# Hybrid transformer block on one core: softmax weights left unscaled in attention, and turned by a product with a diagonal of their factors that GpSimd makes

## The chip, the cores and the metric

The kernel runs on one core of a Trainium2 chip. The metric is the device time of one execution in microseconds. Most executions of it agree within 0.3%.

## The reference, cut to what matters

Two layers work on 768 tokens (256 of context, 512 latent), 1024 channels each. Every layer has three mixers side by side: a two-way recurrence (RWKV-7), grouped attention and a state space model. Their outputs are merged, and a feed-forward block follows. The attention is:

```python
def grouped_attend(q, k, v):
    s = jnp.einsum('bqhgd,bkhd->bhgqk', q, k).astype(jnp.float32) * ATTN_SCALE
    p = jax.nn.softmax(s, axis=-1).astype(v.dtype)
    return jnp.einsum('bhgqk,bkhd->bqhgd', p, v)
```

There are 16 query heads of 64 channels in 4 groups that share keys and values. In both layers the 512 latent queries see all 768 keys. In the first layer alone the 256 context queries see the 256 context keys too.

## The kernel before, in words

Attention is cut into jobs of four query tiles of 128 queries. A latent job (T job) is one head with its four tiles against 768 keys; a context job (C job, first layer only) holds two heads with two tiles each against 256 keys. The first layer has 16 T jobs and 8 C jobs, the second 16 T jobs: 40 in all.

`front` makes the scores of a job in PSUM (`pS`, L1176 and L1177; a T job has its keys in two halves of 384), takes the largest of each row (`st`, L1179), and lets ScalarE write the exponentials into `P` with their row sums (L1180). As each half of a T job is taken against its own maximum, some small operations on `st` (L1184 to L1190) turn sums and maxima into one factor for each row and half, `st[:, 1, y, x]`. A C job needs the reciprocal alone (L1192). Then `P` is multiplied by that factor in place: tiles 0 and 2 on VectorE (L1199), tiles 1 and 3 on ScalarE (L1197).

`back` takes a job's keys 128 at a time (`turn`): TensorE transposes the four tiles of `P` against the identity into one PSUM bank (`pPT`, recorded at L312, the line of a helper that issues calls in a row), ScalarE rounds that to `ph` (L1213), VectorE takes the rest as `pl` (L1214), and two matmuls with `V` add into `pO`. A T job has six turns, 24 transposes; a C job two turns, 8 transposes. With 32 T jobs and 8 C jobs that makes 832 transposes in 208 turns.

`back` of a job and `front` of the next advance by turns. Both are steps of a filler that the recurrence (`rwkv`, its matmuls `pSk`, `pSb`, `pRU`, `pS`, `pY`, and the read-out `rwkv_out` with `pcen`, `pv`, `pr`) calls between its own steps. The attention stage is therefore also that of the recurrence. The order on each engine is made at build time by a scheduler that plays the program through; each engine then runs its own list strictly in that order. GpSimd's list (POOL) holds in this stage the loads of keys, values and queries (`kT`, `kl`, `V`, `qT`), the inverse of small triangular blocks during the recurrence's first step (L1463 and L1465, 62 products and differences in a layer) and the clearing of its results (`XTi`, L1478). TensorE takes float32 operands in `pkb` (L1348), a product of 128x128 by 128 columns in the preparation of the recurrence: 48 calls, and two records for each call in the trace.

Of the kernel before, what the change touches and what calls it, by code (L numbers as in the profile page):

```python
# [8 lines left out]
F32 = mybir.dt.float32  # L9
F32R = mybir.dt.float32r  # L10
I32 = mybir.dt.int32
AF = mybir.ActivationFunctionType
ALU = mybir.AluOpType
# [140 lines left out]
class Net:  # L154
# [975 lines left out]
    def attend(self, l, A, yb, ctx_out, es):  # L1130

        nc, v = self.nc, self.nc.vector
        p = self.pool(f"at_{l}", es=es, side="right")
        pS = self.pool(f"atS_{l}", 2, PSUM, es, side="right")
        pO = self.pool(f"atO_{l}", 1, PSUM, es, side="right")
        ident = self.c["ident"]
        t0 = 0 if ctx_out else TC

        def group(g):
            kT = p.tile([128, T], F32R, name="kT", bufs=2)  # L1140
            nc.gpsimd.dma_start(kT, A["k"][g])
            kl = p.tile([128, T], F32R, name="kl", bufs=2)
            nc.gpsimd.dma_start(kl, A["kl"][g])
            V = p.tile([128, 6, 128], F32R, name="V", bufs=2)
            nc.gpsimd.dma_start(V, A["v"][g])
            return dict(g=g, kT=kT, kl=kl, V=V, qT={}, yo={})
# [10 lines left out]
        def front(g, qts, nk, Ps):  # L1157

            if g not in groups:
                groups[g] = group(g)  # L1160
            G = groups[g]
            qT, kT, kl = G["qT"], G["kT"], G["kl"]
            for h, _ in qts:
                if h not in qT:
                    qT[h] = p.tile([128, T], F32R, name="qT", bufs=3)
                    nc.gpsimd.dma_start(qT[h][:, t0:], A["q"][4 * g + h, :, t0:])
            nh = 2 if nk == T else 1
            w = nk // nh
            st = p.tile([128, 3, nh, 4], F32, name="st", tag=f"st{nh}", bufs=2)
            for x, (h, o) in enumerate(qts):  # L1170
                P = p.tile([128, T], F32, name="P", tag="P", bufs=8)
                Ps.append(P)
                for y in range(nh):
                    ps = pS.tile([128, 512], F32, name="pS", tag="pS")
                    ks = slice(w * y, w * y + w)
                    nc.tensor.matmul(ps[:, :w], qT[h][:, o:o + 128], kT[:, ks], start=True, stop=False)  # L1176
                    nc.tensor.matmul(ps[:, :w], qT[h][:, o:o + 128], kl[:, ks], start=False, stop=True)  # L1177
                    nm, sm, _ = (st[:, z, y, x:x + 1] for z in range(3))
                    v.reduce_max(nm, ps[:, :w], axis=AX.X, negate=True)  # L1179
                    nc.scalar.activation(P[:, ks], ps[:, :w], AF.Exp, bias=nm, accum_out=sm)  # L1180
                yield
            if nh == 2:
                mm = p.tile([128, 2, 4], F32, name="mm", bufs=2)
                v.tensor_tensor(mm[:, 0], st[:, 0, 0], st[:, 0, 1], op=ALU.min)  # L1184
                v.tensor_sub(st[:, 2], mm[:, 0:1].to_broadcast([128, 2, 4]), st[:, 0])
                nc.scalar.activation(st[:, 2], st[:, 2], AF.Exp)
                v.tensor_mul(st[:, 1], st[:, 1], st[:, 2])
                v.tensor_add(mm[:, 1], st[:, 1, 0], st[:, 1, 1])
                v.reciprocal(mm[:, 1], mm[:, 1])
                v.tensor_mul(st[:, 1], st[:, 2], mm[:, 1:2].to_broadcast([128, 2, 4]))  # L1190
            else:
                v.reciprocal(st[:, 1], st[:, 1])  # L1192
            for x in range(4):
                for y in range(nh):
                    ks = slice(w * y, w * y + w)
                    if x % 2:
                        nc.scalar.activation(Ps[x][:, ks], Ps[x][:, ks], AF.Copy, scale=st[:, 1, y, x:x + 1])  # L1197
                    else:
                        v.tensor_scalar(Ps[x][:, ks], Ps[x][:, ks], st[:, 1, y, x:x + 1], None, op0=ALU.mult)  # L1199
            yield  # L1200

        def back(g, qts, nk, Ps):
# [3 lines left out]

            def turn(kt):
                pt = pO.tile([128, 512], F32, name="pPT", tag="pPT", bufs=2)
                self.row_of([self.later(nc.tensor.transpose, pt[:, 128 * x:128 * x + 128],
                                        Ps[x][:, 128 * kt:128 * kt + 128], ident) for x in range(4)])  # L1210
                ph = p.tile([128, 512], F32R, name="ph", bufs=2)
                pl = p.tile([128, 512], F32R, name="pl", bufs=2)
                nc.scalar.copy(ph, pt)  # L1213
                v.tensor_sub(pl, pt, ph)  # L1214
                return ph, pl

            nxt = turn(0)
            for kt in range(nk // 128):
                ph, pl = nxt
# [9 lines left out]
            if nk == T:  # L1229
                if h % 2 == 0:  # L1230
                    yo[h // 2] = p.tile([128, 512], F32, name="yo", bufs=2)
                y = yo[h // 2]
# [3 lines left out]
            else:  # L1236
                y = p.tile([128, 256], F32, name="yoc")
# [8 lines left out]
        for job in jobs + [None]:  # L1246
            Ps = []
# [1043 lines left out]
```

## Time and profile before

| what | value |
|---|---|
| median of 2 runs | 3452.74 us (3449.69 to 3455.78) |
| the profiled execution's own time | 3449.99 us |
| its span, first to last instruction | 3448.1 us |
| mean granted TensorE clock | 0.954 of 2.4 GHz |
| attention with recurrence, first layer | 735 to 1137 us of the span |
| attention with recurrence, second layer | 2570 to 2895 us of the span |

The two stages take 727 of 3448 us. PE is TensorE's matmul, PEld its weight load, DVE is VectorE, ACT ScalarE, POOL GpSimd, SP the engine that issues most DMAs. The end of a matmul is modelled in the trace, so the distance from one start to the next tells more than its duration.

### The profile page before, as it was taken

To read this page: it belongs to the slowest core of one execution; us is meant where nothing else is said; L and a number is where in the kernel's file an instruction comes from. 1 tells how busy PE (TensorE), PEld (TensorE's weight loads), DVE (VectorE), ACT (ScalarE), POOL (GpSimd) and SP (SyncE) were. 2 spreads that over 40 slices of the span, in tenths; PEclk is the share of its full clock that TensorE was granted. 3 is DMA by queue.
4 is the path that set the end of the run, shared out by engine and by line. 5 is a ranking of instruction groups with operands and counts; after the bars stand their busy time and mean duration, and the time that the engine had idled before them with its cause. 6 is when DMAs were issued, how large, how long until landed. Compare 5 with 4: busy or idle time off the path is not lost.

```text
span 3448.1 us, 63260 instructions
## 1 busy us (share of the span) xinstructions
PE 3209.1 (93%) x24501; PEld 2671.1 (77%) x24501; DVE 2217.1 (64%) x4618; ACT 1555.5 (45%) x3166; POOL 524.3 (15%) x746
## 2 busy tenths in 40 slices
PE   7999998979998899999999899978979998999998
PEld 6888897967775789888888787767867775787776
DVE  3889368847778545665455746548858786564446
ACT  3444456656677313422122444436657674243222
POOL 0002022214000030122100221102224000201000
PEclk9999999979999999999999999988969999999999
DMA  5545465675533544344333466637656535544332
GB/s 194 165 135 161 157 186 183 183 204 137 134 93 129 173 130 152 99 147 151 107 109 126 155 207 199 198 110 214 193 169 168 140 86 163 160 152 147 128 128 87
DMA packets 429668, 522.41 MB, mean 152 GB/s; under 512 B 238132, under 2 KB 304820, under 8 KB 428728
## 3 DMA queue, kind: packets, MB, share of 16 engines
q1 hardware_dynamic: 409608, 461.84, 43.9%
q0 software_dynamic: 19760, 56.52, 5.4%
q8 instruction: 194, 3.18, 0.4%
q14 instruction: 106, 0.87, 0.1%
HBM read 372.78 MB, written 145.46 MB: 150 GB/s over the span
## 4 chain that ended last, share of the span: by engine, by line
PE 72%; DVE 10%; DMA 9%; ACT 4%; issue 3%; SPq 1%; POOL 1%; DVEq 0%; ACTq 0%; POOLq 0%
PE pf L343 4%; PE pf L344 4%; PE ph L333 4%; PE pf L345 4%; PE ph L335 4%; PE ph L334 4%; PE pO L312 2%; PE pc L333 2%; PE pga L333 2%; PE pc L334 2%; PE pc L335 2%; PE pga L334 2%; PE pga L335 2%; PE pm L333 2%; PE pm L334 2%
## 5 line engine op out<-in xcount | busy, mean ns | idle before, releaser
L238 ACT CAST whi<-wraw 128x1024 fp32r<-128x1024 f32 x288 | 293.5, 1048 | 571.7 <-PE pf L345 157.5
L239 DVE TENSOR_TENSOR wlo<-wraw,whi 128x1024 fp32r<-128x1024 f32 x288 | 356.0, 1255 | 250.1 <-ACT whi L238 243.9
L333 PE MATMUL ph<-xh,whi 128*128 128x512 f32 (+1 forms) x832 | 287.7, 347 | 4.8 <-DVE xTf L1887 3.6
L334 PE MATMUL ph<-xl,whi 128*128 128x512 f32 (+1 forms) x832 | 286.4, 345 | 0.7 <-DVE xl L1889 0.7
L335 PE MATMUL ph<-xh,wlo 128*128 128x512 f32 (+1 forms) x832 | 285.7, 344 | 0.0
L343 PE MATMUL pf<-whi,hh 128*128 128x512 f32 x640 | 253.4, 397 | 0.7 <-DVE ff L1977 0.3
L344 PE MATMUL pf<-wlo,hh 128*128 128x512 f32 x640 | 252.9, 396 | 0.9 <-DVE wlo L239 0.9
L345 PE MATMUL pf<-whi,hl 128*128 128x512 f32 x640 | 250.7, 396 | 0.0
L1179 DVE TENSOR_REDUCE st<-pS 128x1 f32<-128x384 f32 x288 | 151.7, 535 | 100.9 <-PE pS L1177 98.7
L333 PE MATMUL pga<-xh,whi 128*128 128x512 f32 (+1 forms) x576 | 211.5, 367 | 1.6 <-ACT kT L1063 1.6
L335 PE MATMUL pga<-xh,wlo 128*128 128x512 f32 (+1 forms) x576 | 209.2, 363 | 0.2 <-DVE wlo L239 0.2
L334 PE MATMUL pga<-xl,whi 128*128 128x512 f32 (+1 forms) x576 | 209.2, 363 | 0.0
L1180 ACT ACTIVATE P<-pS,st 128x384 f32<-128x384 f32 x288 | 164.2, 572 | 77.7 <-DVE st L1179 69.5
L1977 DVE TENSOR_TENSOR ff<-ff,pf 128x512 f32<-128x512 f32 x132 | 89.3, 686 | 154.5 <-PE pf L345 154.1
L333 PEld LDWEIGHTS ph<-xh,whi 128*128 128x128 f32 x832 | 157.7, 190 | 30.0 <-issue 6.2
L334 PEld LDWEIGHTS ph<-xl,whi 128*128 128x128 f32 x832 | 158.1, 190 | 22.1 <-DVE xl L1889 1.1
L335 PEld LDWEIGHTS ph<-xh,wlo 128*128 128x128 f32 x832 | 157.7, 190 | 20.4
L1214 DVE TENSOR_TENSOR pl<-pPT,ph 128x512 fp32r<-128x512 f32 x208 | 141.2, 684 | 38.8 <-ACT ph L1213 37.3
L333 PE MATMUL pm<-yh,whi 128*128 128x512 f32 (+1 forms) x384 | 141.7, 373 | 22.1 <-ACT whi L238 16.3
L1176 PE MATMUL pS<-kT,qT 128*128 128x384 f32 x288 | 128.4, 446 | 26.0 <-ACT P L1180 20.6
L343 PE MATMUL pat<-whi,xh 128*128 128x256 f32 x512 | 149.7, 292 | 1.1 <-ACT kT L1063 1.1
L1213 ACT CAST ph<-pPT 128x512 fp32r<-128x512 f32 x208 | 119.4, 588 | 64.8 <-PE pPT L312 55.3
(578 smaller groups left out, 8710.3 us busy)
## 6 DMA issues: line engine op xcount, KB each, us to landing
wraw<-in_mlp_w_dram SPq DMA_DIRECT2D x128, 512.0 KB
wraw<-in_w_in_dram SPq DMA_DIRECT2D x108, 512.0 KB
wraw<-in_mod_w_dram SPq DMA_DIRECT2D x96, 512.0 KB
SUV<-rV SPq DMA_DIRECT2D x192, 64.0 KB
BK<-rBK SPq DMA_DIRECT2D x24, 512.0 KB
rZK<-ZK SPq DMA_DIRECT2D x20, 512.0 KB
Z<-rZK SPq DMA_DIRECT2D x40, 256.0 KB
G<-gst SPq DMA_DIRECT2D x24, 384.0 KB
```

Of the source, the lines that this page charges most:

```text
L238: nc.scalar.copy(h[:, c], r)
L239: nc.vector.tensor_sub(lo[:, c], r, h[:, c])
L333: nc.tensor.matmul(ps, h, a, start=(first and k == 0), stop=False)
L334: nc.tensor.matmul(ps, h, b, start=False, stop=False)
L335: nc.tensor.matmul(ps, lw, a, start=False, stop=(last and k == kt - 1))
L343: nc.tensor.matmul(ps, a, h, start=(k == 0), stop=False)
L344: nc.tensor.matmul(ps, a, lw, start=False, stop=False)
L345: nc.tensor.matmul(ps, b, h, start=False, stop=(k == kt - 1))
L1176: nc.tensor.matmul(ps[:, :w], qT[h][:, o:o + 128], kT[:, ks], start=True, stop=False)
L1179: v.reduce_max(nm, ps[:, :w], axis=AX.X, negate=True)
L1180: nc.scalar.activation(P[:, ks], ps[:, :w], AF.Exp, bias=nm, accum_out=sm)
L1214: v.tensor_sub(pl, pt, ph)
```

## The change

The multiplication of `P` goes away. For each tile GpSimd multiplies the identity, once for each half of the keys, by the factors of that tile: `dg`, 128x256 in a T job and 128x128 in a C job, with eight buffers for each size. `P` stays unscaled, and in place of the transpose there is a float32 matmul with `P` as the stationary and `dg` as the moving operand, which transposes and scales at once.

```diff
             for x in range(4):
-                for y in range(nh):
-                    ks = slice(w * y, w * y + w)
-                    if x % 2:
-                        nc.scalar.activation(Ps[x][:, ks], Ps[x][:, ks], AF.Copy, scale=st[:, 1, y, x:x + 1])
-                    else:
-                        v.tensor_scalar(Ps[x][:, ks], Ps[x][:, ks], st[:, 1, y, x:x + 1], None, op0=ALU.mult)
+                dg = p.tile([128, nh, 128], F32, name="dg", tag=f"dg{nh}", bufs=8)
+                nc.gpsimd.tensor_tensor(dg, ident.unsqueeze(1).to_broadcast([128, nh, 128]),
+                                        st[:, 1, :, x:x + 1].to_broadcast([128, nh, 128]), op=ALU.mult)
+                Ps[x] = Ps[x], dg, w // 128
             yield
...
-                self.row_of([self.later(nc.tensor.transpose, pt[:, 128 * x:128 * x + 128],
-                                        Ps[x][:, 128 * kt:128 * kt + 128], ident) for x in range(4)])
+                self.row_of([self.later(nc.tensor.matmul, pt[:, 128 * x:128 * x + 128], P[:, 128 * kt:128 * kt + 128],
+                                        dg[:, kt // n], start=True, stop=True) for x, (P, dg, n) in enumerate(Ps)])
```

The scheduler lays out all engines' lists anew. On GpSimd, in the first layer just behind the inverse (its last rows are the two of 31 elements), there stood before:

```order
L1463 TENSOR_TENSOR itmp<-NB,D 128x31
L1465 TENSOR_TENSOR D<-D,itmp 128x31
L1166 DMA qT<-aq_995 128x768
L1141 DMA kT<-ak_996 128x768
L1166 DMA qT<-aq_995 128x768
L1143 DMA kl<-akl_997 128x768
L1478 MEMSET XTi 128x512
L1145 DMA V<-av_998 128x768
L1478 MEMSET XTi 128x512 x2
```

At the same place of the changed kernel's GpSimd list (line numbers behind the change are lower by two) there stand now:

```order
L1461 TENSOR_TENSOR itmp<-NB,D 128x31
L1463 TENSOR_TENSOR D<-D,itmp 128x31
L1195 TENSOR_TENSOR dg<-k_ident,st 128x256 x4
L1166 DMA qT<-aq_995 128x768
L1195 TENSOR_TENSOR dg<-k_ident,st 128x256 x4
L1141 DMA kT<-ak_996 128x768
L1166 DMA qT<-aq_995 128x768
L1143 DMA kl<-akl_997 128x768
L1195 TENSOR_TENSOR dg<-k_ident,st 128x128 x4
L1476 MEMSET XTi 128x512 x2
L1145 DMA V<-av_998 128x768
L1476 MEMSET XTi 128x512
```

The diagonals of a job now stand behind loads and memsets that have waits of their own.

On TensorE, at the end of the first layer's stage, the last product of the read-out (`pr<-gd,gup`) had two turns of attention behind it:

```order
L1732 MATMUL pr_13827<-gd,gup 128x256
L312 MATMUL pO<-pl,V 128x512
L312 MATMUL pO<-ph,V 128x512
L312 MATMUL pPT<-k_ident,P 128x128 x4
L312 MATMUL pO<-pl,V 128x512
L312 MATMUL pO<-ph,V 128x512
L312 MATMUL pPT<-k_ident,P 128x128 x4
L312 MATMUL pO<-pl,V 128x512
```

The changed kernel's TensorE list from the same product on:

```order
L1730 MATMUL pr_13859<-gd,gup 128x256
L312 MATMUL pO<-pl,V 128x512
L312 MATMUL pO<-ph,V 128x512
L312 MATMUL pPT<-dg,P 128x128 x8
L312 MATMUL pO<-pl,V 128x512
L312 MATMUL pO<-ph,V 128x512
L312 MATMUL pO<-pl,V 128x512
L312 MATMUL pO<-ph,V 128x512
L312 MATMUL pPT<-dg,P 128x128 x4
L312 MATMUL pO<-pl,V 128x512
L312 MATMUL pO<-ph,V 128x512
L312 MATMUL pPT<-dg,P 128x128 x4
```

After these rows three more of `pPT` x4 follow, one to a turn. Five more turns of attention than before stand behind the read-out.

## Rows read from the trace of the kernel before

**Rows 1.** The page's chain of work that ended last, shares by engine.

```profile
PE 72%; DVE 10%; DMA 9%; ACT 4%; issue 3%; SPq 1%; POOL 1%; DVEq 0%; ACTq 0%; POOLq 0%
```

**Rows 2.** Both stages in five windows: busy us, instructions, TensorE clock, DMA share.

```profile
core 0: us, PE busy (x) PEld busy (x) DVE busy (x) ACT busy (x) POOL busy (x), PEclk, DMA share, GB/s
735.00:790.00 55.00, 48.45 (x458) 37.47 (x458) 42.42 (x94) 34.80 (x91) 13.10 (x28) 0.82 0.68 166
790.00:1042.00 252.00, 234.99 (x3303) 187.39 (x3302) 189.04 (x431) 173.55 (x459) 34.45 (x60) 0.95 0.48 129
1042.00:1137.00 95.00, 81.01 (x352) 50.87 (x352) 87.99 (x198) 67.08 (x166) 0.53 (x1) 0.96 0.30 97
2570.00:2800.00 230.00, 215.15 (x2600) 171.30 (x2598) 183.01 (x417) 168.55 (x433) 46.18 (x87) 0.92 0.57 142
2800.00:2895.00 95.00, 85.33 (x969) 61.99 (x967) 73.44 (x157) 65.42 (x164) 0.53 (x1) 0.94 0.37 111
sum 727.00, PE 664.93 PEld 509.02 DVE 575.90 ACT 509.39 POOL 94.79; mean PE 132.99 PEld 101.80 DVE 115.18 ACT 101.88 POOL 18.96
```

**Rows 3.** The chain by line in the same five windows, in their order.

```profile
by line: PE pSk L312 11.4%; PE pS L1176 11.1%; PE pPT L312 10.8%; DMA BK<-rBK 9.8%; PE pO L312 9.7%; PE pS L1177 7.0%; ACT P L1180 6.6%; issue 6.4%; DVE st L1179 6.0%; DVE Z L1577 5.0%; PE pSb L312 3.8%; PE pBt L312 3.7%; DVE SUV L1662 2.0%
by line: PE pO L312 11.9%; PE pPT L312 8.7%; PE pRU L312 6.5%; PE pSk L312 6.3%; DMA Z<-rZK 6.0%; PE pS L1176 5.3%; PE pS L312 3.9%; PE pY L312 3.8%; DMA rvv<-ry 3.7%; PE pS L1177 3.5%; ACT P L1180 3.4%; PE pSb L312 2.6%; PE pBt L312 2.5%; 
by line: DVE st L1179 11.9%; DVE pl L1214 11.6%; PE pO L312 7.7%; ACT P L1180 5.4%; DVE P L1199 5.4%; PE pPT L312 4.8%; issue 4.5%; DVE yl L1767 3.7%; PE pS L1176 3.5%; ACT ph L1213 3.4%; DVE yacc L1730 3.4%; PE pcen L1709 3.2%; DVE rvv L17
by line: PE pPT L312 9.9%; PE pO L312 9.6%; DMA Z<-rZK 8.7%; PE pS L1176 7.9%; PE pSk L312 6.2%; PE pS L1177 5.1%; PE pRU L312 4.4%; ACT P L1180 4.0%; issue 3.4%; PE pQ L1502 3.3%; PE pQ L1493 3.1%; DVE st L1179 3.0%; PE pBt L312 2.9%; PE p
by line: PE pO L312 14.1%; PE pPT L312 10.2%; PE pY L312 7.3%; PE pRU L312 5.7%; PE pcen L1709 4.9%; PE pS L1176 4.7%; DMA wraw<-in_proj_c_dram 4.5%; PE pv L1713 4.1%; DMA SUV<-rV 4.1%; ACT P L1197 3.7%; DVE pl L1214 3.7%; PE pSk L312 3.4%;
```

**Rows 4.** Transposes and a float32 product of their shape: tile views, then timeline (start, us).

```profile
L312 PE MATMUL pPT<-k_ident,P x832: 270/272/476, 751.0 to 2882.8; 128*128 128x128 f32 x167
921.89 0.60 PE L312 MATMUL pPT<-k_ident,P 128*128 128x128 f32 x4
914.56 1.09 PE L312 MATMUL pPT<-k_ident,P 128*128 128x128 f32 x8
L1348 PE MATMUL pkb<-krsy,k_bind x96: 270/275/377, 451.7 to 2516.9; 128*128 128x128 f32 x96
451.66 1.05 PE L1348 MATMUL pkb<-krsy,k_bind 128*128 128x128 f32 x8
```

**Rows 5.** The scaling's busy time, and what the transposes' tile waited for (us, times).

```profile
sum 727.00, ACT 75.56; mean ACT 37.78
sum 727.00, DVE 52.95; mean DVE 26.47
DVE P L1199: 4.6, 11
ACT P L1197: 3.2, 9
```

**Rows 6.** Timeline of one T job, from its factors to its first transposes.

```profile
2737.76 0.17 DVE L1190 TENSOR_TENSOR st<-st,mm 128x8 f32<-128x8 f32 x1
2737.96 2.14 ACT L1197 ACTIVATE P<-P,st 128x384 f32<-128x384 f32 x4 [1.01 <-DVE st L1190]
2738.74 1.41 DVE L1199 TENSOR_SCALAR P<-P,st 128x384 f32<-128x384 f32 x4
2739.37 1.38 PE L312 MATMUL pPT<-k_ident,P 128*128 128x128 f32 x8
```

**Rows 7.** GpSimd's two-input products in the first stage: busy us, mean ns, idle before.

```profile
L1463 POOL TENSOR_TENSOR itmp<-NB,D 128x252 f32<-128x252 f32 x2 | 1.4, 714 | 0.2
L1463 POOL TENSOR_TENSOR itmp<-NB,D 128x255 f32<-128x255 f32 x2 | 1.4, 678 | 0.2
L1463 POOL TENSOR_TENSOR itmp<-NB,D 128x135 f32<-128x135 f32 x2 | 0.9, 456 | 0.2
```

**Rows 8.** GpSimd's waits over the span: us in total, times, longest.

```profile
POOL qT L1166 <- PE pS L1177: 358.5, 22, 42.2
POOL XTi L1478 <- DMA rXT<-XTi: 68.0, 7, 17.8
```

## The prediction

> **What bounds the kernel now.** I read the chain that ended last first. TensorE holds 72% of it over the whole span [rows 1], so time on TensorE must be argued before time anywhere else. Then I cut the two stages that hold attention into five windows [rows 2]. Matmul records cover 665 of 727 us, VectorE's 576, ScalarE's 509, GpSimd's 95. No engine is full, and GpSimd is nearly empty. One stretch is different: from 1042 to 1137 us, where the recurrence is read out, VectorE is busy for 88 of 95 us.
>
> Which wait ends last is told by the chain in the same windows [rows 3]. The transposes `pPT` are among the six largest lines in each. Their shares make 5.9 + 21.9 + 4.6 + 22.8 + 9.7 = 64.9 us of the path (10.8% of 55 us, 8.7% of 252, 4.8% of 95, 9.9% of 230, 10.2% of 95). The scaling, which the change takes away, is named in two windows alone: 5.4% of 95 us on VectorE and 3.7% of 95 us on ScalarE. So the change lengthens a line that is on the path for some 65 us, and removes one that is there for less.
>
> **The change, part by part.**
>
> *The product in place of the transpose.* There are 832 transposes of 128x128 [rows 4]. One lasts 0.272 us; four in a row cover 0.60 us and eight 1.09, so they start (0.60 - 0.272) / 3 = 0.109 to (1.09 - 0.272) / 7 = 0.117 us apart. I take 0.11, since the eight are two turns with a switch between them. What a float32 product of that shape costs is shown by `pkb`: the same stationary, the same 128 columns, float32 on both sides. Its 48 calls make 96 records, two to a call, and eight records cover 1.05 us with a last one of 0.275: (1.05 - 0.275) / 7 = 0.111 us each, 0.222 us for a call. A product thus takes twice the transpose. On TensorE that adds 832 x 0.11 = 92 us of work. On the path a line that doubles adds what it holds there already, 65 us. The bounds are half of that, 32, if TensorE's gaps take in the rest, and all 92.
>
> A rule of the pages speaks against this change more strongly. The Trainium skill ("TensorE: Matmul & The Clock Gate", section Terms) says that the transpose mode of a load or matmul is four times faster for FP32. By that rule a product would cost 4 x 0.11 = 0.44 us, which adds 832 x 0.33 = 275 us of work and, at the transposes' 65 us on the path, 195 us there. The trace doesn't agree for this shape: the product that it shows is twice as long [rows 4]; the sum goes by that.
>
> *The scaling that goes.* ScalarE loses 75.6 us and VectorE 53.0 us of busy time [rows 5]. The transposes waited little for it, 4.6 + 3.2 = 7.8 us [rows 5]; the rest of its worth is room in two queues. On the path it is 5.1 + 3.5 = 8.6 us where it is named. Elsewhere each of the two lines lies below the smallest share shown, at most 2.0% of 55 us, 2.5% of 252 and 2.9% of 230 [rows 3], and in the windows where one of them is named the other is below 3.2% of 95 and 3.4% of 95. That gives at most 2 x (1.1 + 6.3 + 6.7) + 3.0 + 3.2 + 8.6 = 43 us. Between 9 and 43 I take the middle, 26 us.
>
> *The diagonals on GpSimd.* A T job takes four of 256 columns, a C job four of 128. The nearest rows are the two-input products of the inverse, with broadcast operands too: 0.68 to 0.71 us at 252 and 255 columns, 0.46 at 135, and 0.1 us between two [rows 7]. That makes 128 x 0.7 + 32 x 0.45 = 104 us of work on an engine that is busy for 95 of 727. Beside the path, then, but not beside the job: its factors come from `st`, and the first turn needs all four diagonals. Four at 0.8 us are there 3.2 us after `st`. In the job shown [rows 6] `st` ends at 2737.93, both scalings end at 2740.10 and 2740.15, 2.2 us after. So a T job's first turn comes some 1.0 us later. The transposes were held by the scaling 20 times [rows 5], about half the 40 jobs; half of 32 T jobs at 1.0 us is 16 us. The bounds are 0 (TensorE comes later anyhow) and 32 x 3.2 = 102 us (nothing hides them).
>
> *What the diagonals are queued behind.* GpSimd's list now has them between `qT` loads, which wait for the scores that free their buffer, and `XTi` memsets, which wait for the previous block to be written out. Those waits hurt nobody before. I cost them at nothing: the scheduler sets a load behind the diagonals that are due sooner, and most of the 358 us [rows 8] are waits of an idle engine. If that cover fails, see the first rival. The inverse ends later by the 12 diagonals or so that are mixed into it, 12 x 0.8 = 10 us in a layer; its result is for the recurrence's next steps, and I cost that at nothing too, 10 us a layer at the other end.
>
> *The order on TensorE.* Five more turns of attention stand behind the read-out of the first layer. They are turns that no longer stand before it, in the stretch where VectorE is the bound; I cost that at nothing; its other end is five turns of four products, 5 x 4 x 0.222 = 4 us.
>
> *The clock.* The windows' granted clock of 0.82 to 0.96 [rows 2] means 20 + 25 + 8 + 37 + 11 = 101 us at 1.2 GHz (twice the missing share of each window). Had all of it run at 2.4, TensorE's 72% of the path would gain 101 / 2 x 0.72 = 36 us. Denser work on TensorE may give back a part, but the waits for DMAs that stand on the path remain [rows 3]. I take a quarter, 9 us, of 0 to 36.
>
> The pages have a rule for this too. The Trainium skill ("TensorE: Matmul & The Clock Gate", Part 4) says that transposes don't count as TensorE activity in the way that matmuls do, so that the full clock doesn't engage for them. By it the sum would gain up to the 36 us instead of 9; no row here tells whether a clock fell because of transposes.
>
> **The sum.** 65 - 26 + 16 - 9 = 46 us more than the profiled execution's 3449.99 us, 3496 us. The median of the runs shown is 2.75 us above the profiled one, so the forecast is 3499 us, 1.3% slower. With the terms at moderate distance from their middle it spans 3478 to 3522. About 2%, 69 us, is what a measurement of this kernel can tell from no change, and 3522 is that line.
>
> **The rivals.**
>
> *GpSimd's queue holds the diagonals (slower).* A diagonal that is ready stands behind an `XTi` memset or a `qT` load that is not, TensorE reaches the first product and stops, and the recurrence's matmuls behind it stop too. For it: these waits are 68.0 us in 7 times and 358.5 in 22 times [rows 8], and the list after the inverse puts eight or twelve diagonals behind two such memsets. Against it: the loads wait for scores that come ahead of the diagonals' own. Half of the memsets' 68 us is 34; with a few T jobs that see all 3.2 us of GpSimd's time instead of 1.0, some 16 more, it gives 3549 us. It decides the verdict from 23 us of such waits on.
>
> *TensorE's gaps take it in (no change).* VectorE and ScalarE lose 128.5 us of work [rows 5]; what waited for them comes earlier, and the longer products fill gaps. For it: the matmul records overstate TensorE, and much of the chain goes from engine to engine. Then the product costs 32 us on the path, the scaling gives back 26, the diagonals add 8 or so, and the clock stays: 14 us more, 3467 us. Against it: the scaling was seldom waited for.
>
> *The clock and the freed queues outweigh the product (faster).* With 36 us of clock, 43 us of scaling, the product at 32 and the diagonals at nothing it is 47 us faster, 3406 us. Even this does not reach 69 us.
>
> *The fourfold product (slower).* With 195 us in place of 65 the sum is 3629 us. The shape is the same as that of `pkb`, so I give it little.
>
> **How the numbers follow.** The forecast has 0.51, GpSimd's queue 0.26, no change 0.19, the fourfold product 0.02, faster 0.02. No change, nearly all of the forecast and half of the faster case lie within 2%: 0.70. The queue, the fourfold product and a small part of the forecast's upper end are slower: 0.29. Faster by over 2% would need more than the best of all terms: 0.01. The range goes down to 3450, which leaves out the faster case and the lower part of no change, and up to 3570, above the queue's 3549, which leaves out the fourfold product and a heavier queue: some 0.17 in all.
>
> **What would show it.** In the changed profile `pPT` should have 1664 records, 0.11 us apart; the two stages should be some 45 us longer together, and `pPT`'s share of their chain about twice 65 us. The diagonals should last 0.7 us each, and the first product of a T job should start about 3 us after `st`. VectorE and ScalarE should be 53 and 76 us less busy. Waits of `pPT` for a diagonal of more than 16 us in total would speak for the queue; a clock above 0.96 in all windows for the gate. I am wrong if float32 products of different stationaries don't follow each other at 0.111 us, if the scheduler's list stalls GpSimd, or if the relief of VectorE reaches the path where the table by line doesn't show it.

## The result, and the profile after

The changed kernel takes 3548.95 us (median of 2 runs, 3542.63 to 3555.27) against 3452.74 us: a ratio of 1.0296, with a 95% interval of 1.0254 to 1.0337. It is slower by about 100 us, where 46 us were forecast. The profiled execution took 3555.27 us, 105 us more than the one before; its span is 3553.5 us. One per cent of the time before is 34.5 us, and the ratios below are turned into us by that.

All of it lies in the two attention stages, which were 402 us and 325 us long [rows 2] and are now 462 us and 372 us. These are the windows of after that answer to [rows 2], with edges moved along with the work:

```profile
core 0: us, PE busy (x) PEld busy (x) DVE busy (x) ACT busy (x) POOL busy (x), PEclk, DMA share, GB/s
735.00:790.00 55.00, 31.98 (x296) 26.10 (x294) 22.19 (x46) 15.88 (x44) 20.26 (x40) 0.70 0.78 195
790.00:1088.00 298.00, 286.36 (x3742) 238.99 (x3741) 190.02 (x415) 166.89 (x445) 67.16 (x128) 0.97 0.43 121
1088.00:1197.00 109.00, 96.72 (x497) 71.53 (x496) 85.59 (x179) 59.64 (x148) 14.74 (x25) 0.94 0.26 83
2630.00:2900.00 270.00, 246.44 (x2954) 206.72 (x2955) 174.15 (x378) 148.43 (x392) 79.55 (x144) 0.93 0.52 132
2900.00:3002.00 102.00, 89.62 (x969) 70.90 (x966) 61.86 (x131) 56.78 (x141) 9.93 (x17) 0.93 0.32 96
sum 834.00, PE 751.13 PEld 614.23 DVE 533.83 ACT 447.62 POOL 191.63; mean PE 150.23 PEld 122.85 DVE 106.77 ACT 89.53 POOL 38.33
```

TensorE's matmul records grew by 751 - 665 = 86 us while VectorE and ScalarE lost 42 and 62 us. The clock gave nothing back: the shares that it lacks come to 2 x (0.30 x 55 + 0.03 x 298 + 0.06 x 109 + 0.07 x 270 + 0.07 x 102) = 116 us at 1.2 GHz, against 101 us before. The first window shows something that the forecast has no term for: TensorE is busy there for 32 of 55 us, where it was for 48.

The chain by line in the whole of the first stage and of the second, as in [rows 3]:

```profile
by line: PE pPT L312 19.6%; PE pO L312 10.9%; DMA Z<-rZK 7.2%; PE pRU L312 6.3%; PE pS L1176 5.7%; PE pSk L312 4.7%; PE pY L312 4.4%; PE pS L1177 3.8%; PE pS L312 3.0%; DVE st L1179 2.0%; DMA XT<-rXT 2.0%; PE pBt L312 2.0%; PE pSb L312 1.8%
...
by line: PE pPT L312 22.7%; PE pO L312 14.3%; PE pRU L312 7.8%; PE pS L1176 7.2%; PE pS L1177 5.4%; PE pY L312 5.3%; PE pSk L312 4.9%; PE pS L312 3.7%; DMA SUV<-rV 2.8%; PE pBt L312 2.7%; DMA Z<-rZK 2.3%; issue 2.1%; DMA rvv<-ry 1.9%; PE pS
```

`pPT` holds 19.6% of 462 us and 22.7% of 372 us, 175 us in all, where it held 65 us. The scaling lines have gone, and `st` has shrunk. So did the waits on GpSimd's diagonals take the time? The tile `pPT` (matmul records, the two readers, and what TensorE and the readers waited for: us, times):

```profile
L312 PE MATMUL pPT<-dg,P x1664: 270/275/582, 771.5 to 2991.4; 128*128 128x128 f32 x185
L1211 ACT CAST ph<-pPT x208: 568/586/642, 774.2 to 2991.7; 128x512 fp32r<-128x512 f32 x104
L1212 DVE TENSOR_TENSOR pl<-pPT,ph x208: 661/684/694, 775.2 to 2993.8; 128x512 fp32r<-128x512 f32 x104
its engine sat idle before it (us, times) until:
  PE pPT L312: 123.3, 114
  ACT ph L1211: 81.0, 63
  POOL dg L1195: 5.0, 5
```

No. In 208 turns TensorE waited for a diagonal 5 times, 5.0 us together, its weight loads counted in. The readers `ph` and `pl` wait for TensorE. GpSimd's own rows (the diagonals and what they waited for, then the rows that answer to [rows 8]) say the same: it waits for the factors, and the wait for scores on its list has become shorter.

```profile
L1195 POOL TENSOR_TENSOR dg<-k_ident,st x160: 392/613/1411, 770.8 to 2973.0; 128x256 f32<-128x256 f32 x128, 128x128 f32<-128x128 f32 x32
its engine sat idle before it (us, times) until:
  DVE st L1190: 243.4, 25
```

```profile
POOL qT L1166 <- PE pS L1177: 156.1, 17, 20.9
...
POOL XTi L1476 <- DMA rXT<-XTi: 74.9, 10, 16.2
```

One T job in order of time, as [rows 6]: the factors are ready at 2703.42, four diagonals take 2.35 us, and the first product starts at 2706.41, 3.0 us behind the factors. The eight records of the job's first turn come in three pieces with other matmuls between them. The last piece, four records that are two calls, covers 0.61 us: they follow each other 0.11 us apart, as those of `pkb` do [rows 4].

```profile
2703.25 0.17 DVE L1190 TENSOR_TENSOR st<-st,mm 128x8 f32<-128x8 f32 x1
...
2703.56 2.35 POOL L1195 TENSOR_TENSOR dg<-k_ident,st 128x256 f32<-128x256 f32 x4 [0.81 <-DVE st L1190]
...
2706.41 0.38 PE L312 MATMUL pPT<-dg,P 128*128 128x128 f32 x2
...
2707.77 0.61 PE L312 MATMUL pPT<-dg,P 128*128 128x128 f32 x4
```

What is late is the start. Before the change GpSimd's list, in order of time, loads the first keys right behind the second `XTi` memset:

```profile
710.16 0.53 POOL L1478 MEMSET XTi<- 128x512 f32 x1 [11.78 <-PE pQ L1493]
719.73 0.53 POOL L1478 MEMSET XTi<- 128x512 f32 x1 [9.04 <-PE pQ L1493]
720.21 0.61 POOL L1141 DMA_DIRECT2D kT<-ak  x1
```

In the changed kernel three memsets come first, and then the load waits for 7.91 us more:

```profile
712.96 0.53 POOL L1476 MEMSET XTi<- 128x512 f32 x1 [13.48 <-DMA rXT<-XTi]
720.98 0.53 POOL L1476 MEMSET XTi<- 128x512 f32 x1 [7.49 <-PE pQ L1491]
730.32 0.53 POOL L1476 MEMSET XTi<- 128x512 f32 x1 [8.81 <-DMA rXT<-XTi]
738.75 0.61 POOL L1141 DMA_DIRECT2D kT<-ak  x1 [7.91 <-DMA SUV<-rV]
```

Behind the last `pkb` of a layer's preparation the first `pS` started 60.5 us later in the first layer and 51.8 us later in the second; it is now 71.9 us and 71.2 us. Attention starts 11 and 19 us late. The profile puts the load's wait down to the loads `SUV<-rV`; the last write-out of `XTi` was issued on the same queue, SP's, 0.38 us ahead of the first of them (736.05 and 736.43).

The two programs place `kT` at different bytes of a partition (the places are read from the programs as built; a trace has none). Attention's pool grows downwards from its place on the right side of the memory, and in the first layer the sixteen `dg` buffers take 8 x 1024 + 8 x 512 bytes = 12 KB of it:

```
first layer     first kT buffer   lies on
before          161376            araw, last used long before
changed         149088            XTi and D1 of the preparation's inverse, in use until the end
```

The second layer has no C jobs, so its pool grows by 8 KB. That puts the first key buffer on `QT`, another tile of the inverse.

### The profile page after: what moved, and what is told of

Read it like the earlier page. It is cut to its first block, busy times and chain, and to the rows that moved or that the text cites. A ratio compares the mean times of both kernels' runs of the same rounds, so it can differ in the third digit from the quotient of the medians.

```text
span 3553.5 us, 64954 instructions
## 1 busy us (share of the span) xinstructions
PE 3292.0 (93%) x25333; PEld 2776.5 (78%) x25333; DVE 2173.9 (61%) x4474; ACT 1494.0 (42%) x3022; POOL 613.0 (17%) x906
## 4 chain that ended last, share of the span: by engine, by line
PE 61%; DMA 7%; DVE 6%; issue 3%; ACT 2%; SPq 1%; POOL 0%; POOLq 0%; DVEq 0%; ACTq 0%
PE pPT L312 5%; PE ph L333 4%; PE pf L343 4%; PE pf L344 4%; PE ph L335 4%; PE ph L334 4%; PE pf L345 4%; PE pO L312 3%; PE pm L333 2%; PE pm L334 2%; PE pm L335 2%; PE pRU L312 2%; PE pS L1176 1%; DMA Z<-rZK 1%; PE pSk L312 1%
## 5 line engine op out<-in xcount | busy, mean ns | idle before, releaser
L312 PEld LDWEIGHTS pPT<-dg,P 128*128 128x128 f32 x1664 | 224.4, 195 | 21.5 <-POOL dg L1195 2.9
L312 PE MATMUL pPT<-dg,P 128*128 128x128 f32 x1664 | 235.7, 282 | 2.1 <-POOL dg L1195 2.1
```

What stands on the lines that cost most here:

```text
L312: return lambda: f(*a, **kw)
```

## The experiments

Every ratio is to the kernel before on the same chip, with its 95% interval.

**The product and the scaling apart.** Two theories stood against each other. By A, TensorE has become the bound and the product's whole 92 us arrive. By B, the product costs what was forecast and the excess comes with GpSimd's diagonals. Four kernels split the change. The first drops the scaling and keeps the transposes:

```diff
-                for y in range(nh):
-                    ks = slice(w * y, w * y + w)
-                    if x % 2:
-                        nc.scalar.activation(Ps[x][:, ks], Ps[x][:, ks], AF.Copy, scale=st[:, 1, y, x:x + 1])
-                    else:
-                        v.tensor_scalar(Ps[x][:, ks], Ps[x][:, ks], st[:, 1, y, x:x + 1], None, op0=ALU.mult)
```

> Leaves out the softmax factors altogether: P stays unscaled, nothing is made of them, and the transposes stay transposes. It gives the most that taking the scaling away can bring. Theory A (after the change TensorE is the bound, so the product's whole work of some 92 us arrives and the room in the other queues is worth nothing there): the gain by itself is what the path showed, 9 to 43 us, so 3410 to 3445 us. Theory B (the excess over the forecast comes from GpSimd: its diagonals arrive late or disturb VectorE): says the same here.

The second also replaces the transpose by a product with the identity:

```diff
-                self.row_of([self.later(nc.tensor.transpose, pt[:, 128 * x:128 * x + 128],
-                                        Ps[x][:, 128 * kt:128 * kt + 128], ident) for x in range(4)])
+                self.row_of([self.later(nc.tensor.matmul, pt[:, 128 * x:128 * x + 128],
+                                        Ps[x][:, 128 * kt:128 * kt + 128], ident, start=True, stop=True) for x in range(4)])
```

> Leaves out the softmax factors as well; the transposes become float32 products with the identity, so GpSimd makes nothing. Theory A: nearly all of the excess stays, 3525 to 3555 us, and some 90 to 120 us above the kernel with neither scaling nor products. Theory B: without diagonals only the doubled path share is left, 3470 to 3500 us.

The third has that product alone, with the scaling of before.

> Complete computation: the scaling of before stays on VectorE and ScalarE, and the transposes become float32 products with the identity. Theory A: the relief of VectorE and ScalarE is worth little once TensorE is the bound, so the time lies near the changed kernel's, 3540 to 3575 us. Theory B: no GpSimd work, so the product's 65 us on the path alone, about 3518 us, and below the changed kernel.

The fourth has the change in tiles 1 and 3 alone (four `dg` buffers of each size), and in tiles 0 and 2 VectorE's scaling and the transposes.

> Complete computation: tiles 1 and 3 go by the product with a diagonal from GpSimd, tiles 0 and 2 are scaled on VectorE and transposed. Half of TensorE's additional work, ScalarE's scaling gone. Theory A: as long as TensorE has gaps the product fills them, so less than half of the change's 96 us is paid, 3470 to 3500 us. A rival to it, that the cost grows in proportion to the products: 3501 us. Theory B: half of the diagonals, 3495 to 3505 us, with waits of pPT for dg in the trace.

| kernel | time | ratio | against before |
|---|---|---|---|
| no scaling | 3403.5 us | 0.9873 (0.9841 to 0.9905) | -44 us |
| no scaling, product with the identity | 3472.9 us | 1.0073 (1.0048 to 1.0099) | +25 us |
| scaling and product with the identity | 3491.0 us | 1.0131 (1.0105 to 1.0158) | +45 us |
| half | 3472.8 us | 1.0080 (1.0053 to 1.0108) | +28 us |

Theory A falls: the product adds 25 + 44 = 69 us without the scaling and 45 us with it, not 92. Of its forecasts only the half's came true. Theory B's came true for the product with the identity; the kernels without scaling and with scaling and product came out faster than either theory had them. The scaling is worth 44 us beside transposes and 20 us beside products.

The first two kernels lack more than the scaling. Their turns don't wait for the factors: by their traces 31 of 32 T jobs start the first turn before the operation that makes the factors (L1190) has ended, in the mean 9.9 us ahead of it without scaling and 7.3 us ahead with the product. The changed kernel can't have that, as its products wait for the factors through the diagonals. Between the product with the identity (+25 us) and the whole change (+102 us) lie 77 us that must come from the diagonals (their making, the wait for them, the memory they take) or from the wait for the factors. The half came out below what theory B expects: it makes half of the diagonals and has hardly any of the excess. None of these four kernels takes 12 KB (the half takes 6), and all of them start attention as early as before (first `pS` 59 to 61 us and 50 to 53 us behind the last `pkb`).

**The memory, the making and the wait.** By theory C the 12 KB are most of it. By rival D the late start is taken in by later gaps. The first kernel is the one before with 12 KB held and never touched:

```diff
             for x in range(4):
+                if nk not in held:
+                    held[nk] = p.tile([128, 8, nh, 128], F32, name="held", tag=f"held{nh}")
                 for y in range(nh):
```

> The kernel before with 12 KB per partition held in attention's pool and never touched, as much as the changed kernel's diagonals take; no instruction differs from before. Theory C (the diagonals' memory moves the first key buffer onto tiles that the preparation still uses, and attention starts 11 us and 20 us late in the two layers): the first pS behind the last pkb at 72 us and 71 us, as in the changed kernel, against 60.5 us and 51.8 us, and the time up by most of 31 us, 3470 to 3490 us. Rival D (the late start is taken in by later gaps, and what is left of the loss is the transposes' dependence on GpSimd's four diagonals of each job): the time within 5 us of before, 3443 to 3455 us, wherever attention starts.

It took 3474.8 us, 1.0073 (1.0051 to 1.0096), +25 us, for memory that nothing reads or writes. GpSimd's list in order of time has the shape of the changed kernel's, to the 7.93 us of wait:

```profile
706.97 0.53 POOL L1480 MEMSET XTi<- 128x512 f32 x1 [11.53 <-DMA rXT<-XTi]
717.05 0.53 POOL L1480 MEMSET XTi<- 128x512 f32 x1 [9.56 <-DMA rXT<-XTi]
725.58 0.53 POOL L1480 MEMSET XTi<- 128x512 f32 x1 [8.01 <-ACT QT L1500]
734.04 0.61 POOL L1141 DMA_DIRECT2D kT<-ak  x1 [7.93 <-DMA SUV<-rV]
```

The first `pS` comes 70.6 us and 68.7 us behind the last `pkb`. The second kernel is the changed one with 6 KB:

```diff
-                dg = p.tile([128, nh, 128], F32, name="dg", tag=f"dg{nh}", bufs=8)
+                dg = p.tile([128, 2, 128], F32, name="dg", tag="dg", bufs=6)[:, :nh]
```

> The changed kernel with six diagonal buffers shared by both kinds of job, 6 KB per partition in place of 12 KB; the first key buffer then lies on memory that was used last long before. Theory C: attention starts as in before (60 us and 52 us behind the last pkb), and the time falls by most of 31 us, to 3510 to 3530 us. Rival D: the start is early, the time stays at 3540 to 3560 us, since each job still waits for its diagonals; six buffers might add waits of GpSimd for a free buffer.

It took 3511.0 us, 1.0185 (1.0149 to 1.0220), +64 us: 38 us less than the changed kernel. Its first key buffer lies at byte 155232, clear of the inverse, and its GpSimd list has the load behind the second memset again, with the first `pS` at 59.7 and 52.1 us:

```profile
718.28 0.53 POOL L1476 MEMSET XTi<- 128x512 f32 x1 [7.61 <-DMA rXT<-XTi]
718.75 0.61 POOL L1141 DMA_DIRECT2D kT<-ak  x1
```

In the third, the products of that kernel read the identity and the diagonals are made for nobody (`dg[:, kt // n]` becomes `ident`).

> As the one with six buffers, but the products read the identity, so that GpSimd makes the diagonals and nobody reads them; the softmax's factors are left out of the result. It is the product with the identity (3472.9 us) plus GpSimd's work on its list. Theory C with GpSimd's list free: 3470 to 3480 us. If GpSimd's work itself costs (loads queued behind diagonals, memory taken from others): 3490 to 3510 us. The gap from here to the kernel with six buffers is the price of waiting for the diagonals: under rival D 60 us or more, under theory C 30 to 50 us.

It took 3474.9 us, 1.0077 (1.0055 to 1.0098), +27 us. That is 1 us over the product with the identity that has no diagonals at all, so GpSimd's work costs nothing where nobody waits for it, and the loads behind the diagonals on its list cost nothing either. Reading the diagonals, and with them waiting for the factors, costs 64 - 27 = 37 us. Unread, 30 of 32 T jobs start the first turn ahead of their factors, 6.9 us in the mean. These rows are of the first job of that trace:

```profile
742.96 3.27 PE L312 MATMUL pPT<-k_ident,P 128*128 128x128 f32 x16
...
746.56 0.17 DVE L1190 TENSOR_TENSOR st<-st,mm 128x8 f32<-128x8 f32 x1
```

Since the kernel with six buffers differs in the number of buffers too, the memory was later tried once more on a version with few, large diagonals (below), three buffers of 2 KB against six:

> The kernel that makes the diagonals by halves (ratio 1.011), with six buffers of 2 KB in place of three, so that attention's pool is as large as the changed kernel's, 12 KB over before. If the memory's place is the cause of the late start: the first pS 72 us and 71 us behind the last pkb again, against 60 us and 52 us, and 25 to 38 us more (25 with the untouched 12 KB in the kernel before, 38 between the changed kernel and the one with six buffers), 3508 to 3522 us. If the number of buffers was what helped or hurt: within 8 us of 3483, or faster, since twice the buffers can only take waits away.

It took 3522.6 us, 1.0221 (1.0183 to 1.0259), against 1.0110 with three buffers: +38 us again, with more buffers and no other edit. The first `pS` is at 71.8 and 72.6 us. Rival D falls, and theory C's price in the changed kernel is 38 us.

**The wait for the factors.** By theory L the 37 us are the time from the factors to the first turn. By rival S they are the small operations on `st` ahead of it, which no maker of diagonals changes. A third reading is the order: a scheduler that sees the first turn ready later puts other matmuls ahead of it. A turn is four calls. Turns that stand on TensorE's list ahead of the first `pr` of the first layer's read-out, of 112:

```
before                        89      changed                  84
no scaling                   104.75   scaling and product      90
product with the identity    106      diagonals made, unread  106
six buffers                   86      six, on VectorE          96.5
halves first                  89      six, more turns          92
12 KB held                    84
```

Three kernels start from the one with six buffers. In the first VectorE makes the diagonals (`nc.gpsimd` becomes `v`).

> The kernel with six diagonal buffers (3511 us), its diagonals made by VectorE, which also makes the factors, so that nothing passes between engines and four follow each other faster. Theory L (the 36 us between that kernel and the one whose products read the identity are the time from factors to first product, paid in nearly every job): 3480 to 3500 us, in spite of some 50 us of added work on VectorE. Rival S (the 36 us are the small operations on st, which stand between the sums and the factors and which the product with the identity doesn't wait for): no gain from a nearer maker, 3505 to 3530 us.

In the second GpSimd makes all four tiles of one half in one operation:

```diff
-            for x in range(4):
-                dg = p.tile([128, 2, 128], F32, name="dg", tag="dg", bufs=6)[:, :nh]
-                nc.gpsimd.tensor_tensor(dg, ident.unsqueeze(1).to_broadcast([128, nh, 128]),
-                                        st[:, 1, :, x:x + 1].to_broadcast([128, nh, 128]), op=ALU.mult)
+            for y in range(nh):
+                dg = p.tile([128, 4, 128], F32, name="dg", tag="dg", bufs=3)
+                nc.gpsimd.tensor_tensor(dg, ident.unsqueeze(1).to_broadcast([128, 4, 128]),
+                                        st[:, 1, y].unsqueeze(2).to_broadcast([128, 4, 128]), op=ALU.mult)
...
```

> The kernel with six diagonal buffers, but GpSimd makes the diagonals of all four tiles of one half of the keys in one operation of 512 columns, the first half's first; the memory is the same. The first product of a T job then waits for one operation, about 1.05 us (0.39 us for 128 columns and 0.61 for 256 continue to that), in place of four that take 2.35 us. Theory L: 1.3 us less in 32 jobs are up to 41 us; with half of it on the path 3485 to 3500 us. Rival S: within 6 us of 3511, 3505 to 3517 us.

In the third the recurrence calls the filler more often:

```diff
-NC0, NC1 = (3, 3, 3, 3), (2, 3, 3, 2)
+NC0, NC1 = (4, 4, 4, 4), (3, 4, 4, 3)
```

> The kernel with six diagonal buffers, in which the recurrence calls the attention filler four times for each of its steps in place of three (in the second layer 3, 4, 4, 3 in place of 2, 3, 3, 2). On TensorE's list 92 of 112 turns then stand ahead of the first layer's first read-out product, against 86 (89 before the change, 106 where the products read the identity). If the order on TensorE's list is how the diagonals cost time: six turns of 2.0 to 2.7 us, 12 to 16 us less, 3494 to 3500 us. If the products wait as long wherever they stand (theory L at run time): 3505 to 3520 us.

VectorE as the maker gave 3485.9 us, 1.0124 (1.0105 to 1.0143): 21 us less than with GpSimd, though VectorE got 160 operations more. Halves first gave 3483.4 us, 1.0110 (1.0087 to 1.0132): 26 us less. More turns gave 3499.1 us, 1.0160 (1.0140 to 1.0179): 9 us less by the ratios, with intervals that overlap. The diagonals' durations in the two that gained (min, median, max in ns), VectorE's first:

```profile
L1195 DVE TENSOR_TENSOR dg<-k_ident,st x160: 273/416/949, 749.2 to 2909.2; 128x256 f32<-128x256 f32 x128, 128x128 f32<-128x128 f32 x32
```

```profile
L1196 POOL TENSOR_TENSOR dg<-k_ident,st x72: 1029/1039/1424, 749.1 to 2906.4; 128x512 f32<-128x512 f32 x72
```

Rival S can't be the whole: it expected no gain, as the operations on `st` are the same in all of them. It keeps a part, since 11 to 16 of the 37 us are left, and the scaling of before, which waits for the same factors, costs 45 - 25 = 20 us beside products.

Theory L holds in its direction and size. Diagonals that are there 4 x (0.61 - 0.42) = 0.8 us or 2.35 - 1.04 = 1.3 us sooner give 21 to 26 us in 32 T jobs. The traces show the first turn of a job come sooner too. This is the time from the end of L1190 to the start of the last of the first turn's four calls, added over the 32 T jobs, in us:

```
before                       101     six buffers            136
scaling and product          105     six, on VectorE        108
changed                      133     halves first           118
```

GpSimd's waits for a free diagonal buffer rose from 13.8 us (once) in the changed kernel to 65.2 us (14 times) with six buffers. They are not what halves first gains from: with 12 KB, where it has six large buffers, it is ahead of the changed kernel by the same 26 us (1.0296 against 1.0221).

But on the chip the products wait little for diagonals, 5.0 us in the changed kernel and 12.3 us with six buffers:

```profile
its engine sat idle before it (us, times) until:
...
  POOL dg L1195: 12.3, 8
```

So most of the 37 us is not paid as a stop at the first product. The table of turns speaks for the order, where later turns are moved behind the read-out and run there with little beside them; the kernel with more turns points the same way, by a gain that is not clear of the noise. The layers tell a part of it apart. In the profiled executions of the kernels with six buffers and with unread diagonals, 25 of 34 us have come by the last `pkb` of the second layer, and 9 come after it. In that layer all 96 turns stand ahead of the first `pr` in both, so the order behind the read-out has no part in those 9. How much of the 25 is order and how much is wait was not measured apart.

**Versions that might beat both.** One took ScalarE's scaling of tile 3 to GpSimd, as one pass over the tile:

```diff
+                if x == 3:
+                    P3 = Ps[x][:, :nk].rearrange("p (y k) -> p y k", y=nh)
+                    nc.gpsimd.tensor_tensor(P3, P3, st[:, 1, :, x:x + 1].to_broadcast([128, nh, w]), op=ALU.mult)
+                    continue
```

> The kernel before, with the fourth query tile of each job scaled by GpSimd's tensor_tensor in place of ScalarE's two activations; transposes stay. If the scaling's 44 us (time before less the time without any scaling) are ScalarE's and VectorE's work in equal parts, a quarter of it goes: 3430 to 3445 us. If a job's transposes wait for the slowest tile, GpSimd's one pass of 768 columns (some 2 us by its 0.59 us for 256) comes later than ScalarE's two, and 32 jobs lose some 0.5 to 1 us each: 3460 to 3480 us.

It took 3477.7 us, 1.0080 (1.0057 to 1.0104), +28 us, in the range that the slowest tile was to give. But the slowest tile is not GpSimd's: its pass over 768 columns has a median of 1.54 us and ends 1.8 us behind the factors in the median. VectorE's scalings end last, at 2.8 us, where they ended at 1.7 before. Those that the pass doesn't touch last 0.41 us (97 of them), those that it covers for more than half of their time 1.06 us (46). TensorE waited for them for 20.9 us, where it was 4.6 [rows 5], and no row of `pPT` has it wait for the pass. The rows show one T job, what `pPT` waited for, and the durations (min, median, max in ns; GpSimd's with both shapes):

```profile
2704.29 0.16 DVE L1190 TENSOR_TENSOR st<-st,mm 128x8 f32<-128x8 f32 x1
...
2704.60 1.47 POOL L1196 TENSOR_TENSOR P<-P,st 128x768 f32<-128x768 f32 x1 [3.90 <-DVE st L1190]
...
2705.27 2.00 DVE L1203 TENSOR_SCALAR P<-P,st 128x384 f32<-128x384 f32 x4
...
  DVE P L1203: 20.9, 31
...
L1203 DVE TENSOR_SCALAR P<-P,st x144: 334/407/1629, 747.7 to 2897.9; 128x384 f32<-128x384 f32 x128, 128x256 f32<-128x256 f32 x16
...
L1196 POOL TENSOR_TENSOR P<-P,st x40: 603/1469/2821, 747.8 to 2895.8; 128x768 f32<-128x768 f32 x32, 128x256 f32<-128x256 f32 x8
```

One changed the order of the scaling in the kernel before, to the first half of all four tiles and then the second (`for y` outside `for x`).

> The kernel before, with the scaling in another order: the first half of the keys of all four tiles, then the second half, so that a T job's first turn waits for two scalings on each engine and not for three. If the time from factors to first turn is paid in nearly every job: some 0.5 us less in 32 jobs, up to 16 us, 3430 to 3440 us, a version that beats both. If the list on TensorE decides (87 turns ahead of the first read-out product, against 89 before): no gain or a small loss, 3445 to 3455 us.

It took 3450.7 us, 1.0013 (0.9994 to 1.0031): nothing. What helped with diagonals doesn't help here, where the turn waited for the scaling 7.8 us in all [rows 5] and the list changed by two turns. The first turns of the T jobs came no sooner: by the measure of the table above they make 113 us, where they made 101. One did without diagonals and without the wait:

```diff
+                    if y:
+                        v.tensor_tensor(nm, nm, st[:, 0, 0, x:x + 1], op=ALU.min)
...
+            rw = self.dp.tile([4, 128], F32, name=f"rw{l}_{g}_{qts[0][0]}_{nh}")
+            nc.sync.dma_start(rw.rearrange("x p -> p x"), st[:, 1, 0])
...
+                nc.sync.dma_start(fb[64 * (h % 2):64 * (h % 2) + 64], rw.rearrange("x p -> (x p)").partition_broadcast(64))
...
+                nc.gpsimd.tensor_tensor(y[o], y[o], factors[g, h, nk][o], op=ALU.mult)
```

> A version that needs neither the diagonals nor the wait: the transposes of before; the second half of the keys is taken against the larger of both maxima, its turns come first, only the first half is scaled, by the ratio of the two maxima, and the division by the sum is made at the job's end, on GpSimd, by a row that a DMA spreads over the partitions. If what scaling costs before is the wait between factors and first turn: most of the 44 us that leaving it out gains, 3410 to 3430 us. If it is the work on VectorE and ScalarE: half of 44 less some 10 us for the added small operations, 3430 to 3445 us. If the spread row comes late at the job's end or the second maximum delays the exponentials: 3450 us or more.

It took 3603.0 us, 1.0459 (1.0438 to 1.0481). The waits of the DMA queue of SP over the span, then two of GpSimd in the first stage (us, times, longest):

```profile
SPq L1200 <- DMA rw<-st: 238.5, 31, 9.5
...
POOL yo L1242 <- DVE yo L1241: 99.8, 4, 31.4
...
POOL yo L1242 <- DMA fb<-rw: 68.7, 5, 18.9
```

The load of the spread row waits on SP's queue until the row has been written out, 7.7 us each time, and the recurrence's loads stand behind it on that queue. Without the row and the division:

> The version with the division at the job's end, without the row, its DMAs and GpSimd's product: the division by the sum is left out of the result. If the row was the loss (its DMAs stand on SP's list among the recurrence's loads, its product waits on GpSimd ahead of query loads): 3405 to 3430 us. If the second maximum, which is now in front of the second half's exponential, was the loss: 3500 us or more.

It took 3455.4 us, 1.0019 (0.9998 to 1.0040). So the row and what hangs on it cost some 150 us (SP's wait and GpSimd's product were not told apart), and the scheme of the two maxima by itself gains nothing: by the ratios it is 50 us short of leaving all the scaling out. Why it gains nothing is open. No version here beats the kernel before.

## Why the prediction was wrong, step by step

| step | priced (bounds), us | measured, us | by |
|---|---|---|---|
| the scaling that goes | -26 (-43 to -9) | -44, with the wait for the factors | no scaling against before |
| the product | +65 (32 to 92) | +69 | product with the identity against no scaling |
| making the diagonals, loads behind them on GpSimd's list | 0 | +1 | unread diagonals against none |
| waiting for factors and diagonals | +16 (0 to 102) | +37 | six buffers against unread diagonals |
| memory of the diagonals | no term | +38 | changed against six buffers; twice |
| the clock | -9 (-36 to 0) | no gain seen | granted clock of the windows |
| sum | +46 | +101 | +102 by the ratio |

The measured steps lead from the kernel before to the changed one, so that they add up is no check of them. The -44 and the +37 don't answer to -26 and +16 one by one, as the kernels between them don't wait for the factors. Through kernels that all wait for them the steps are: the product +45 (forecast 65), the diagonals in place of the scaling 64 - 45 = +19 (forecast -26 + 16 = -10), the memory +38 (no term).

**The step that failed** first is one that isn't there: the memory, 38 of the 56 us by which the change came out dearer than the sum. The forecast counted instructions, waits and queue places, and costed "what the diagonals are queued behind" at nothing. It never asked where sixteen buffers of memory come from. 12 KB more in attention's pool put the first key buffer on tiles of the preparation, and the scheduler set the load behind them. GpSimd's list was read behind the inverse, where the diagonals begin, and not at the head of the stage, where no diagonal stands yet and the loss begins. The untouched 12 KB in the kernel before and the pair of kernels with three and six large buffers show it as a cause.

**The second** is the exchange of the scaling for the diagonals, forecast as a gain of 10 us and measured as a loss of 19. I took a first turn that comes 1.0 us later in half of 32 T jobs. With six buffers its last call starts (136 - 101) / 32 = 1.1 us later than before in the mean of all of them. The reason that I gave is not the one: the four diagonals are there 2.5 us behind the factors in the median, not 3.2, hardly later than the last scaling before the change (2.4). But the first turn needs the first half of the keys alone, and ScalarE's last scaling is for the second half. The kernel that makes the first half's diagonals 1.3 us sooner won 26 us, 0.8 us in every T job. How much of the loss is wait and how much the order on TensorE's list stays open.

**The product** was right: 1664 records, 0.11 us apart; of 92 us 69 reach the path without the scaling and 45 with it, within the bounds. **The scaling** is worth 20 us beside products, near the 26. The 44 us beside transposes are one over the bound. The shares of the chain show who ended a wait, while the going of the scaling and of the wait for the factors moves 16 turns ahead of the read-out on TensorE's list (89 to 104.75), which no share of a chain tells. So the terms are not independent.

**GpSimd's queue** is the rival whose 3549 us is the time that came, and that is luck, since its mechanism is refuted. It asked for over 16 us of waits of `pPT` for a diagonal, and there are 5.0; in the changed kernel's trace no job has its first diagonal start more than 0.8 us behind the factors. **TensorE's gaps** took in 23 of 92 us (47 with the scaling kept), not 60. **The clock** went from 101 to 116 us missing, so the quarter that I took has no support; all transposes of attention are gone, and its windows are granted 0.93 to 0.97 behind the first one, where 0.92 to 0.96 were. The two kernels without scaling, one with transposes and one with products, have a mean granted clock of 0.962 and 0.963. By the rule of the Trainium skill ("TensorE: Matmul & The Clock Gate", Part 4) that transposes don't count as activity it should have risen; these rows show no such rise. **The fourfold product** did not occur: a call has two records where the transpose had one, at the same distance. The fourfold rate that the Trainium skill gives to transposes ("TensorE: Matmul & The Clock Gate", Terms) is a twofold one here.

## What to carry to other kernels

Before a change adds buffers, find where the pool that grows puts its first tiles: 12 KB that nothing touched cost 25 us by holding the next stage's first loads behind the last one's tiles, and halving the buffers gave back 38 us. A dependency that the scheduler sees changes the order too: look at what moved behind the end of the stage, not only for waits at the new consumer. What the first consumer needs should be made first and in few operations, and a load that waits for a write of the same queue should not stand on the queue that feeds the critical recurrence.

## What the runs showed of the hardware that was not expected

GpSimd's product of two operands grows less than in proportion: 0.40 us at 128 columns, 0.61 at 256, 1.04 at 512, so one of 512 replaces two of 256 (1.2 us) or four of 128 (1.6 us) at a gain. The inverse's rows of 0.68 to 0.71 us at 252 and 255 columns [rows 7] were 0.1 us too high for it. VectorE needs 0.42 us for the same 256 columns. Beside GpSimd's pass over `P`, VectorE's scaling of `P` lasted 1.06 us in place of 0.41, while its maximum of the scores, which it reads from PSUM, lasted 0.55 us with and without the pass. A write of 512 single factors to memory kept the next load on its queue waiting for 7.7 us (238.5 us in 31 times).
